# Copying the first sixteen right half rows of a half-matrix swap in uneven 4 KB strips

## The chip, the core and the metric

The kernel runs on one core of a Trainium2 chip. The metric is the device time of one execution in microseconds. The kernel uses no compute engine: it consists of copies from device memory to device memory. Two instruction queues issue them, that of SyncE (SP) and that of ScalarE (ACT), and the core's 16 DMA engines carry them out.

## The reference

The input is a matrix of 8192 x 8192 float32 numbers (268 MB). The output is the same matrix with both axes rotated by half their length, so that the four quadrants change places diagonally:

```python
def reference(x):            # x: (8192, 8192) float32
    return np.fft.ifftshift(x)
```

## The kernel before

R and C are 8192, hr and hc are 4096. A row of the output consists of a left and a right half row, each of 4096 numbers or 16 KB that lie together. The source of an output half row is the half row that lies hr rows and hc columns away (modulo the size). So the whole job is 16384 copies of 16 KB.

`ENGINES` is 16 and `per` is 16, so `rows` is 256: one DMA copies 256 half rows, 4 MB. The helper `copy(queue, row, col, dims)` issues one DMA at L29. It computes the source's place from the output's row and column, and uses the same list of steps and counts, `dims`, on both sides. The list is `back`:

```python
back = [[C, ENGINES], [-ENGINES * C, per], [1, hc]]
```

The outermost step has the count 16 and goes from one row to the next, one row for each DMA engine. The second goes back by 16 rows, 16 times: within a DMA each engine takes every sixteenth row of the block, from the block's end to its start. The innermost runs along one half row, which is one packet of 16 KB.

The outer loop takes `first` from the matrix's end to its start in steps of four blocks (1024 rows). Within a step `n` counts down from 3 to 0. SP's queue copies the left half of block n, and ACT's queue the right half of block (n + 2) % 4. The blocks of the first step of ACT are therefore 1, 0, 3, 2 of the last 1024 rows. The block with which ACT begins starts at row R - 3 * rows.

There are 64 DMAs, 32 from each queue. The framework gives them eight completion semaphores in turn, and an issue waits until the earlier DMA on its semaphore has landed. As built, ACT's issues use semaphores 0, 2, 4 and 6, SP's use 1, 3, 5 and 7. So each queue issues four DMAs at once, and each further one when its own fourth-last has landed. A DMA counts as landed when all 16 DMA engines have reported their part. No DMA depends on another one's data.

Of the kernel before, what the change touches and what calls it, by code (L numbers as in the profile page):

```python
# [1 line left out]

# [4 lines left out]


ENGINES = 16


@with_exitstack
def kernel(
    ctx: ExitStack,
    tc: tile.TileContext,
    x: bass.AP,
    out: bass.AP,
):
    nc = tc.nc
    R, C = x.shape  # L20
    hr = R // 2
    hc = C // 2
    per = 16
    rows = ENGINES * per

    def copy(queue, row, col, dims):

        src = (row + hr) % R * C + (col + hc) % C
        queue.dma_start(  # L29
            out=bass.AP(out.tensor, out.offset + row * C + col, dims),  # L30
            in_=bass.AP(x.tensor, x.offset + src, dims),
        )

    back = [[C, ENGINES], [-ENGINES * C, per], [1, hc]]

    for first in range(R - 4 * rows, -1, -4 * rows):
        for n in (3, 2, 1, 0):
            copy(nc.sync, first + n * rows + rows - ENGINES, 0, back)
            copy(nc.scalar, first + (n + 2) % 4 * rows + rows - ENGINES, hc, back)


# [1 line left out]
_INS = ['x']  # L43
_OUTS = [((8192, 8192), 'float32')]


def kernel(**inputs):
    import numpy as _np
    import concourse.bacc as _bacc
    import concourse.tile as _tile  # L50
    from concourse import mybir as _mybir
    from concourse.bass_utils import run_bass_kernel_spmd as _run

    nc = _bacc.Bacc("TRN2", target_bir_lowering=False, num_devices=1)  # L54
    arrays, args = {}, []
    for name in _INS:
        a = _np.ascontiguousarray(inputs[name])
        if a.dtype.kind in "iu":
            a = a.astype(_np.int64)
        arrays[f"in_{name}_dram"] = a  # L60
        args.append(nc.dram_tensor(f"in_{name}_dram", a.shape, _mybir.dt.from_np(a.dtype), kind="ExternalInput").ap())
    for i, (shape, dtype) in enumerate(_OUTS):
        dt = _mybir.dt.from_np(_np.dtype(dtype))
        args.append(nc.dram_tensor(f"out_{i}_dram", shape, dt, kind="ExternalOutput").ap())
    with _tile.TileContext(nc) as tc:
        kernel(tc, *args)
    r = _run(nc, [arrays], core_ids=[0])
    got = tuple(r.results[0][f"out_{i}_dram"] for i in range(len(_OUTS)))
    return got[0]
```

## Time and profile before

| What | Value |
|---|---|
| Median of 3 runs | 814.51 us (814.3 to 814.64) |
| Profiled execution | 813.9 us |
| Its span, first to last instruction | 812.1 us |
| Data moved | 268.44 MB, mean 331 GB/s |
| DMA issues | 64, of 4096 KB each |
| Issue to landing, median | 101.0 us |

The profile's rate counts each byte once. Reading and writing together are 661 GB/s. The two queues appear in it as q1 and q10. "DMA share" is the busy time of the 16 DMA engines, as a part of a stretch. "L65" in the waits is the end of the program, where it waits for the last transfers.

### The profile page before, as it was taken

Reading aid. Unit: us, or ns where it says so; the run is one execution under the profiler, and the core shown is the slowest. Engines: PE = TensorE matmul, PEld = TensorE weight load, DVE = VectorE, ACT = ScalarE, POOL = GpSimd, SP = SyncE. Lnnn points to the kernel's source line nnn. Section 1 sums busy time; section 2 is a strip of 40 time slices with the busy share of each in tenths; the row PEclk is TensorE's granted clock in tenths of the full one; section 3 lists DMA queues with packets and bytes.
Section 4 is the critical chain, followed back from the end, with each engine's and each line's share of the span. In section 5 each row is a group of like instructions: output and inputs, shape, how many; then the busy total and the mean of one; then the engine's idle time right before and its main releaser. Section 6 shows DMA issues by size and latency. Waiting matters only on the chain. (4 is left out here: it accounts for less than half of the span.)

```text
span 812.1 us, 109 instructions
## 1 busy us (share of the span) xinstructions
POOL 0.2 (0%) x4
## 2 busy tenths in 40 slices
POOL 0000000000000000000000000000000000000000
DMA  9999999999999999999999999999999999999998
GB/s 306 332 329 337 333 332 335 328 324 337 329 336 337 332 334 334 334 336 331 332 329 330 337 328 334 339 331 333 332 320 333 330 331 330 336 332 337 334 333 286
DMA packets 17408, 268.44 MB, mean 331 GB/s; under 512 B 1024, under 2 KB 1024, under 8 KB 1024
## 3 DMA queue, kind: packets, MB, share of 16 engines
q1 hardware_dynamic: 8704, 134.22, 49.9%
q10 hardware_dynamic: 8704, 134.22, 49.1%
HBM read 268.44 MB, written 268.44 MB: 661 GB/s over the span
## 5 line engine op out<-in xcount | busy, mean ns | idle before, releaser
L54 POOL MEMSET const-bfloat16-1.0<- 128x1 bf16 x1 | 0.1, 102 | 0.0
L54 POOL MEMSET const-uint8-127<- 128x1 uint8 x1 | 0.1, 102 | 0.0
L54 POOL MEMSET const-float32-1.0<- 128x1 f32 x1 | 0.1, 99 | 0.0
L54 POOL MEMSET const-float32-0.0<- 128x1 f32 x1 | 0.1, 98 | 0.2 <-issue 0.2
## 6 DMA issues: line engine op xcount, KB each, us to landing
out_dram<-in_x_dram ACTq DMA_DIRECT2D x32, 4096.0 KB, 101.0
out_dram<-in_x_dram SPq DMA_DIRECT2D x32, 4096.0 KB, 101.0
```

The costliest lines, as they stand in the source:

```text
L54: nc = _bacc.Bacc("TRN2", target_bir_lowering=False, num_devices=1)
```

## The change

ACT's first copy took 256 right half rows of the block that starts at `start` = R - 3 * rows, from the block's end to its start. Its first sixteen half rows, one for each DMA engine, are now copied separately, before everything else. They are cut into four strips of 1024 columns, 4 KB a row. Three strips go in two DMAs each: 14 rows and 2 rows, 9 and 7, 4 and 12. The fourth goes in one DMA of 16 rows. ACT's large copy of that block then does the remaining 15 times 16 half rows (`rest`); all other copies stay as they were.

So ACT issues 39 DMAs instead of 32. The seven small ones come first on its queue. If each row of a small DMA goes to a DMA engine of its own, counted from the first one, the sixteen engines get 7, 7, 6, 6, 5, 5, 5, 4, 4, 3, 3, 3, 2, 2, 1 and 1 strips; each had one half row, four strips' worth, before.

The eight semaphores are given out in the program's order. The seven strips take 0 to 6, SP's first large copy takes 7. As built, ACT's first four large copies wait for the strips on 0, 2, 4 and 6 (14, 9, 4 and 16 rows). SP's second, third and fourth copies wait for the strips on 1, 3 and 5 (2, 7 and 12 rows), and its fifth for its first. After that each queue again waits for its own fourth-last DMA.

```diff
+    start = R - 3 * rows
+    strip = hc // 4
+    for n, k in enumerate((14, 9, 4)):
+        col = hc + n * strip
+        copy(nc.scalar, start + rows - ENGINES, col, [[C, k], [1, strip]])
+        copy(nc.scalar, start + rows - ENGINES + k, col, [[C, ENGINES - k], [1, strip]])
+    copy(nc.scalar, start + rows - ENGINES, hc + 3 * strip, [[C, ENGINES], [1, strip]])
+
     back = [[C, ENGINES], [-ENGINES * C, per], [1, hc]]
-
+    rest = [[C, ENGINES], [-ENGINES * C, per - 1], [1, hc]]
     for first in range(R - 4 * rows, -1, -4 * rows):
         for n in (3, 2, 1, 0):
             copy(nc.sync, first + n * rows + rows - ENGINES, 0, back)
-            copy(nc.scalar, first + (n + 2) % 4 * rows + rows - ENGINES, hc, back)
+            right = first + (n + 2) % 4 * rows
+            if right == start:
+                copy(nc.scalar, right + rows - 2 * ENGINES, hc, rest)
+            else:
+                copy(nc.scalar, right + rows - ENGINES, hc, back)
```

## The prediction

> **What bounds the kernel now.** I read the page's summary of slices and queues first, then the queue's own waits, then the line that issues the copies, and last the windows at the two ends and along the middle. No compute engine works (POOL 0.2 us of 812.1), so the chain that ended last says nothing here; the transfer rows carry it. From the page:
>
> ```profile
> DMA  9999999999999999999999999999999999999998
> GB/s 306 332 329 337 333 332 335 328 324 337 329 336 337 332 334 334 334 336 331 332 329 330 337 328 334 339 331 333 332 320 333 330 331 330 336 332 337 334 333 286
> DMA packets 17408, 268.44 MB, mean 331 GB/s; under 512 B 1024, under 2 KB 1024, under 8 KB 1024
> q1 hardware_dynamic: 8704, 134.22, 49.9%
> q10 hardware_dynamic: 8704, 134.22, 49.1%
> HBM read 268.44 MB, written 268.44 MB: 661 GB/s over the span
> ```
>
> The sixteen DMA engines are busy in all 40 slices; the two queues share them evenly (49.9% and 49.1%, together 99%). Only the first slice (306) and the last (286) fall off. 17408 packets are 16384 half rows of 16 KB and 1024 small ones that signal completion (64 DMAs times 16). The span is therefore 16384 / 16 = 1024 half rows per DMA engine at 99% of 812.1 / 1024 = 0.785 us each. The packet records give the same: mean 784 ns, least 608, longest near 2.3 us. The least is an undisturbed packet; the 176 ns above it are contention, and that alone is what a change of phase could touch.
>
> Now who waits. These are SP's queue waits, then what all instructions of the copy's line show:
>
> ```profile
> SPq L29 <- DMA out_dram<-in_x_dram: 689.7, 28, 25.2
> SPq L65 <- DMA out_dram<-in_x_dram: 101.6, 2, 79.3
> ...
> L29 ACTq DMA_DIRECT2D out_dram<-in_x_dram x32: 577/578/884, 0.7 to 713.4; - x32
> L29 SPq DMA_DIRECT2D out_dram<-in_x_dram x32: 571/571/666, 0.7 to 709.0; - x32
> ...
> DMA to landing us min/median/max: 25.4/101.0/103.2
> ```
>
> SP waits 28 times for a DMA four places back, 689.7 us in total, and issues the next in 571 ns. Each transfer lands a median 101 us after its issue: four are outstanding on each queue, and each queue issues only once in some 25 us, so issuing is well covered. Next the start and the end: transfers of the stretches 0 to 5 us and 807 to 809 us by queue, then rates by window (microseconds, POOL busy, clock, DMA share, GB/s; a packet counts where it starts, so a short window can pass 1.00):
>
> ```profile
> q1 hardware_dynamic: 64, 1.05, 58.6%
> ...
> q10 hardware_dynamic: 39, 0.56, 91.1%
> q1 hardware_dynamic: 7, 0.00, 0.2%
> ...
> 2.20:5.00 2.80, 0.00 (x0) 1.00 1.00 363
> 12.00:25.00 13.00, 0.00 (x0) 1.00 0.99 325
> 50.00:100.00 50.00, 0.00 (x0) 1.00 1.00 337
> 250.00:300.00 50.00, 0.00 (x0) 1.00 0.99 334
> 600.00:650.00 50.00, 0.00 (x0) 1.00 1.00 328
> 700.00:750.00 50.00, 0.00 (x0) 1.00 1.00 333
> 808.00:809.00 1.00, 0.00 (x0) 1.00 0.75 197
> 809.00:810.00 1.00, 0.00 (x0) 1.00 0.31 131
> ```
>
> SP's queue (q1; its DMAs land first) moves alone until 5 us: first packet at 2.18 us, ACT's at 5.08, though both were issued at 0.73. At the end ACT's queue (q10) is alone, and the engines finish one by one between 808.7 and 810.9 us. In the middle, fifteen windows of 50 us lie between 328 and 337 GB/s, mean 332.6, without a trend.
>
> **The change, part by part.** The sum is made against the profiled execution: 813.9 us, that is a span of 812.1 and 1.8 around it. The median of the runs, 814.5, stands 0.6 above it.
>
> *Bytes and packets.* The same 268.44 MB. Sixteen packets of 16 KB become 64 of 4 KB, with 64 small ones for seven more DMAs. The trace has no 4 KB packet. Between the rows for 4 B (9 ns) and 16 KB (608 ns) a straight line gives 159 ns; four are 636 in place of 608, and four extra signals per engine 36: 0.06 us per engine. Upper bound: every strip suffers the full 176 ns that a 16 KB packet does, 4 x 335 = 1.34 against 0.784: 0.56 us. Lower bound: a quarter of 608 each, no change. I take **+0.1**, near the straight line, since the strips run while only one other stream is live.
>
> *Seven more issues on ACT.* The first issues took 0.67 to 0.88 us, and followed one another at about 0.7: seven take 4.9 us. ACT's large copy, now 15 rows per engine, goes out near 5.7 us and its packets start near 10 instead of 5.08. What hides this is SP's first DMA: 16 half rows per engine from 2.18 us, at no less than 0.61 each, so until 12 us at least, with 2.5 us of strips beside it. Without that cover it would cost the 4.9 us. Queued behind the strips on ACT are its 32 large copies; the first four of these wait for strips, and SP's second to fifth copies for strips two, four, six and its own first copy. All those strips land long before 12 us, so nobody starves: cost **0**, upper bound 1 us if ACT's descriptors come as late after their issue as in the before (4.35 us) and SP's later ones get in front.
>
> The Trainium skill's page "DMA: Bandwidth & Descriptors", section "Rules for kernel authors", speaks against this part: small transfers are to be merged, as below 64 KB one pays mostly overhead. By its table of measured sizes (0.68 us for 4 KB, 0.95 for 64 KB) seven strips in a row would be an estimated 6 us if exposed; the row of q1 above, engines fed by the other queue, says they are not.
>
> *The lag of the two streams.* SP is alone for longer, and so is ACT at the end. Before, SP got 64 / 16 = 4 half rows per engine ahead. With ACT's bulk at 10 us it gets about (10 - 2.2 - 0.6) / 0.67 = 11, less the one that the strips cover: 6 more than before, at each end. Counted by each packet's share in a stretch, they run at some 390 GB/s from 3 to 5 us, 0.67 us each, from 806 to 808 at some 370, against 0.79 with both. Were that due to the lone stream, 12 half rows x 0.12 = 1.4 us would be saved; if it is a start and an end effect, nothing. One-microsecond windows scatter widely: I take **-0.4**.
>
> *Unlike amounts.* With one row per engine, counted from the first, engines get 7,7,6,6,5,5,5,4,4,3,3,3,2,2,1,1 strips. The mean is 4, what each had before. The first two carry 12 KB too much: 12.3 KB at 331 / 16 = 20.7 GB/s is 0.59 us, or 3 x 159 ns = 0.48. It costs this in full if these engines are the last anyway, and less if a lighter one is: between -0.59 and +0.59, and as the kernel ends with its slowest engine, I take **+0.3**.
>
> *The middle.* Would unlike starts change the 784 ns? Two readings say no. Completions of one DMA over the 16 engines spread 1.1 to 1.6 us for the first four DMAs, 2.2 to 2.5 for the last four, while the windows show no trend: engines drift apart by more than a half row without becoming faster. And from 3 to 5 us they start almost together, and run fastest. One reading says yes: sorting stretches of 5 us by how far the running packets are in step, those less in step are faster, but weakly (correlation 0.22); in-step-ness itself is forgotten within 1 us (autocorrelation 0.05). I take **0**; the windows set the bounds, 328 and 337.
>
> The same page, section "Latency and other measured facts", holds a rule for the change: copies with a row pitch of 512 KiB run at 207 GB/s, of 4 MiB at 103, and padding the latter by 4 KiB gives 214; the page infers that streams in step meet in the same channel. The pitch here is 32 KB and the rate 331, and no run here shows such a collapse. By that rule, at its extreme, every packet could come down to its least, 608 ns, an estimated 632 us; by the rows of the middle the sum gets nothing.
>
> Sum: 813.9 + 0.1 + 0 - 0.4 + 0.3 + 0 = 813.9, no change; at the median 814.5.
>
> **The rivals.** *Forecast* (0.52): the middle keeps its pace, and only ends move; its own range is 813.0 to 816.2. *Faster* (0.26): engines keep their spacing over the run and meet less often. For it: the weak sorting above, and that spacing of one DMA's completions grows by only 1 us in 800, so a spacing that is set at the start could last. Against: the loss of step within 1 us. Price: the mean rises from 332.6 to 334.5 GB/s, as several windows have: 0.57% or 4.6 us, 809.9. *Slower* (0.20): ACT's stream runs 6 half rows per engine further behind, so the two streams read and write other pairs of row blocks at any moment over the whole run. For it: windows at 328 and 330 show that some pairings are worse; against: no trend. It decides once the mean is below 331.9 (0.2%); at 331, half way to the worst windows, it is 0.48% or 3.9 us: 818.4. *The change doesn't do what it says* (0.02): small DMAs aren't dealt a row per engine; then the amounts are other ones, and the time is that of the forecast or, if seven or nine rows share an engine, 8 x 0.159 = 1.3 us more.
>
> **How the numbers follow.** A measurement of this kernel tells about 0.2%, 1.6 us, from no change. The forecast's case lies almost wholly within that: with its edges same 0.50, faster 0.28, slower 0.22. The range takes in the faster rival at 809.9 and most of the slower one: 809.5 to 818.0.
>
> **What would show it.** Right: 71 issues on L29, 39 from ACT; about 17520 packets, 1152 of them under 8 KB; q10 with packets soon after 2.2 us, its 16 KB ones from some 10 us on; SP's wait near 690 us; windows of 50 us around 332.6; a lone q10 at the end for 3 to 4 us longer than now. Wrong, term by term: a window before 15 us below 300 GB/s (cover failed); last engines ending over 3 us apart (the amounts add up); every window of the middle at 334 or more, or at 331 or less (a rival).

## The result, and the profile after

The changed kernel took 811.4 us (median of 18 runs, 809.33 to 814.68) and the kernel before 814.15 us in the same comparison (18 runs, 810.02 to 817.91): ratio 0.9968, 95% interval 0.9955 to 0.9981. Three more comparisons on other chips gave 0.9982 (0.9969 to 0.9996), 0.9989 (0.9970 to 1.0007) and 0.9989 (0.9972 to 1.0006). Weighted by the inverse squares of their intervals' widths the four are 0.9980 (0.9972 to 0.9987): 1.6 us less, just where a measurement begins to tell it from no change. The three later ones alone give 0.9986 (0.9977 to 0.9995). The other chips run both kernels about 1% slower (before: 822 us), so only ratios within a chip are compared below. All comparisons on one chip share the same runs of the kernel before (29 to 35), so an error of these runs is in all of them.

The profiled execution took 812.7 us, its span is 810.9. First the page's rows for the slices and the queues:

```profile
GB/s 302 328 335 329 334 333 331 331 335 330 326 331 329 331 335 330 332 332 337 335 336 333 333 337 330 334 335 331 336 331 333 335 334 335 333 330 336 333 338 296
DMA packets 17520, 268.44 MB, mean 331 GB/s; under 512 B 1088, under 2 KB 1088, under 8 KB 1152
q1 hardware_dynamic: 8704, 134.22, 49.7%
q10 hardware_dynamic: 8816, 134.22, 49.6%
```

The packets are the foreseen ones: 64 strips under 8 KB, 64 more completion signals. The first slice is no better than before (302, it was 306); the last is (296, it was 286). Next SP's queue waits, the size and landing of the one strip DMA that uses all sixteen engines, and the queues from 16.5 to 20.5 us:

```profile
SPq L29 <- DMA out_dram<-in_x_dram: 686.8, 28, 28.4
...
out_dram<-in_x_dram ACTq DMA_DIRECT2D x1, 64.0 KB, 10.8
...
q10 hardware_dynamic: 77, 1.26, 97.4%
q1 hardware_dynamic: 17, 0.08, 5.8%
```

From 16.5 to 20.5 us SP's queue is all but empty. The text ahead of the prediction, and the prediction after it, had the semaphores wrong. By the issue records SP's first copy took the second semaphore, not the eighth, so SP's second copy waited for its first, which landed at 19.23 us, and was issued at 19.25. The nine-row, four-row and sixteen-row strips held SP's next three copies, and the fourteen-row, two-row, seven-row and twelve-row strips ACT's first four, not the ones named. It cost nothing, since ACT's large copy was there. These are the windows of the start (microseconds, POOL busy, clock, DMA share, GB/s):

```profile
5.00:10.00 5.00, 0.00 (x0) 1.00 1.04 337
10.00:15.00 5.00, 0.00 (x0) 1.00 1.02 333
15.00:20.00 5.00, 0.00 (x0) 1.00 1.00 333
20.00:25.00 5.00, 0.00 (x0) 1.00 0.96 315
25.00:30.00 5.00, 0.00 (x0) 1.00 1.02 334
```

There is no hole. Up to 50 us 15.70 MB had been moved, before 15.66: 0.1 us of gain at most. The middle, from 50 to 780 us, of the kernel before and then of the changed one:

```profile
50.00:780.00 730.00, 0.00 (x0) 1.00 1.00 333
```

```profile
50.00:780.00 730.00, 0.00 (x0) 1.00 1.00 333
```

To whole GB/s the same in this pair. Counted from the packet records it is 332.5 before and 332.7 after, which is 0.5 us over 730. The end differs more. Here are the stretches from 5 to 3 and from 3 to 1 us before the end of the span, before and then after:

```profile
807.10:809.10 2.00, 0.00 (x0) 1.00 0.89 270
809.10:811.10 2.00, 0.00 (x0) 1.00 0.16 66
```

```profile
805.90:807.90 2.00, 0.00 (x0) 1.00 0.94 319
807.90:809.90 2.00, 0.00 (x0) 1.00 0.32 115
```

Before, in the second stretch, the engines are busy for a sixth of the time: most have finished and wait for a few. After, for a third. By the completion records of the last DMA, the last engine ended 1.33 us behind the mean of the sixteen before, and 0.82 after.

### The profile page after: what moved, and what is told of

Its sections match the earlier page's. It is cut to its first block, busy times and chain, and to the rows that moved or that the text cites. A ratio compares the mean times of both kernels' runs of the same rounds, so it can differ in the third digit from the quotient of the medians.

```text
span 810.9 us, 116 instructions
## 1 busy us (share of the span) xinstructions
POOL 0.2 (0%) x4
```

## The experiments

Three theories were set against each other. A: the unlike amounts keep the engines apart. B: SP's stream leads ACT's by more, so other blocks meet all along. C: the gain is made at the start and the end, where one stream runs alone. Later D: the order of issues and semaphores does it. "Lead" is SP's bytes minus ACT's, in half rows per engine, at 400 us of the profile: 3.5 before, 5.4 after.

**First chip of three: the changed kernel again, and three that part strips, amounts and lead.**

e1_same is the changed kernel.

> The changed kernel once more, as the yardstick for the three others on this chip. All theories: 2 to 3.5 us below the kernel before (ratio 0.9957 to 0.9975), SP's stream 5 to 6 half rows per engine ahead of ACT's in the middle of the run where it was 3.5 before.

Measured: 821.31 us, ratio 0.9982 (0.9969 to 0.9996), lead 5.0: 1.7 us below before, less than was expected.

e2_even7 makes the amounts equal:

```diff
-    strip = hc // 4
-    for n, k in enumerate((14, 9, 4)): ...
+    strip = hc // 8
+    for n in range(7):
+        wide = strip if n < 6 else 2 * strip
+        copy(nc.scalar, start + rows - ENGINES, hc + n * strip, [[C, ENGINES], [1, wide]])
```

> Seven small DMAs again, but each of all 16 rows (six of 2 KB and one of 4 KB a row): same number of issues and same order of semaphores, no unlike amounts. Theory A (unlike amounts keep the engines apart): the gain is gone, within 1 us of the kernel before. Theory B (ACT's stream starts later, so SP leads by some two half rows more for the whole run): the gain stays, 2 to 3.5 us below, as the lead will be 5 half rows or more. Theory C (the gain is made in the first 30 us and at the end, by stretches with one live stream): it stays too, and the middle is at the pace of before.

Measured: 821.25 us, ratio 0.9986 (0.9973 to 0.9999), lead 7.8. The gain did not go with the unlike amounts, against A; but its last engine, 1.83 us behind the mean, ended later than before's (1.33), so it was worth repeating.

e3_even16 cuts the first half rows into 16 even strips:

```diff
-    strip = hc // 4
-    for n, k in enumerate((14, 9, 4)): ...
+    strip = hc // 16
+    for n in range(16):
+        copy(nc.scalar, start + rows - ENGINES, hc + n * strip, [[C, ENGINES], [1, strip]])
```

> The first sixteen half rows in 16 even strips of 1 KB: ACT's bulk starts later still. A: no gain, and up to 1 us lost to more issues. B: the lead grows beyond 6 half rows and the time goes further, some 1 us from the changed kernel either way. C: more of the start with one stream, 3 to 5 us below the kernel before.

Measured: 829.31 us, ratio 1.0083 (1.0063 to 1.0103), lead 24.1. All theories missed. The windows of its start:

```profile
10.00:15.00 5.00, 0.00 (x0) 1.00 0.96 315
15.00:20.00 5.00, 0.00 (x0) 1.00 0.09 26
20.00:25.00 5.00, 0.00 (x0) 1.00 0.84 276
```

Here the hole opens which the changed kernel avoids. By the issue records ACT's ninth strip shares its semaphore with SP's first copy: it was issued at 16.79 us, when that copy had landed at 16.77. SP's second copy shares one with ACT's tenth strip, which landed at 19.35, and was issued at 19.37. So each queue waited for the other with almost nothing under way; ACT's bulk was issued at 21.83 and moved its first packet at 29.3. The missing share is (329 - 26) / 329 x 5 = 4.6 us and (329 - 276) / 329 x 5 = 0.8 us: 5.4 us. The median lost 6.3 (822.99 to 829.31), this execution, which took 827.86, some 4.9.

e4_lead has no strips; one half row per engine goes from SP to ACT:

```diff
+    copy(nc.scalar, R - ENGINES, 0, [[C, ENGINES], [-ENGINES * C, 1], [1, hc]])
...
+            if left == R - rows:
+                copy(nc.sync, R - 2 * ENGINES, 0, rest)
```

> No strips at all. ACT copies the first sixteen of SP's half rows as a first DMA, and SP's first block begins one half row per engine further on: SP's stream leads by two half rows more over the whole run, 5.5 in place of 3.5, with equal amounts on all engines and the start of before. A: no gain, within 1 us of before. B: the full gain, 2 to 3.5 us. C: at most 0.5 us, from the longer lone stream at the end.

Measured: 823.32 us, ratio 1.0007 (0.9990 to 1.0024). ACT's short first DMA got its packets out first, at 2.14 us, so the lead in bytes was only 2.4. In place it is 4.4, since SP's stream begins one half row further on and one of ACT's was not of its own stream: short of the 5.5 meant. No gain, but a weak test of B.

**Second chip: the amounts enlarged, and the order of issues alone.**

> The changed kernel a third time, for a joint interval and a further profile. All theories: ratio 0.996 to 0.9985. Theory A (unlike amounts) and B (longer lead of SP's stream) put the gain into the middle, theory C into the last 30 us, so its end (from 780 us on, beyond the time that the bytes left need at the pace of the middle) shows under 0.6 us lost where before lost 0.9.

Measured (the changed kernel): 821.77 us, ratio 0.9989 (0.9970 to 1.0007), a little less gain than expected. From 780 us on it moved 12.55 MB, at its middle pace of 329.4 GB/s worth 38.1 us, in 38.9: 0.8 us lost, so not below the 0.6 that was expected.

> Seven even small DMAs once more, since the first time left both open (ratio 0.9973 to 0.9999). A: joint ratio with the first time nearer to 1 than to the changed kernel's. B and C: the same ratio as the changed kernel's on this chip, within 0.1%.

Measured (even strips once more): 821.65 us, ratio 0.9990 (0.9979 to 1.0001); joint with the first 0.9988 (0.9980 to 0.9997).

f3_rows4 splits whole half rows as the change splits strips:

```diff
-        copy(nc.scalar, start + rows - ENGINES, col, [[C, k], [1, strip]]) ...
+        row = start + rows - (n + 1) * ENGINES
+        copy(nc.scalar, row, hc, [[C, k], [1, hc]])
+        copy(nc.scalar, row + k, hc, [[C, ENGINES - k], [1, hc]])
```

> The same split of 14 and 2, 9 and 7, 4 and 12, 16, but of whole half rows of 16 KB (the first 64 half rows of ACT's block): the amounts differ by up to six half rows in place of six strips. A with spacing in time: a larger gain than the changed kernel's, 4 us or more. A with fractions of a packet only: none. If the unequal shares stay with their engines to the end, the first two engines end 3 x 0.78 = 2.3 us behind the mean and the kernel is 1 to 3 us slower than before. B: SP's lead is about that of before (full packets), so no gain.

Measured: 822.72 us, ratio 1.0015 (1.0000 to 1.0030), lead 2.2. The large amounts do not help the middle, which speaks against a spacing in time. What they do is seen at the end:

```profile
814.60:816.60 2.00, 0.00 (x0) 1.00 0.53 213
816.60:818.60 2.00, 0.00 (x0) 1.00 0.14 57
```

Already five to three microseconds before the end nearly half of the engine time is gone. The sixteen engines ended over 5.17 us (2.0 to 3.8 in the kernels with equal amounts); their amounts differed by six half rows, 6 x 0.79 = 4.7 us. The completion records show it all along. A queue that shares the engines gets half of their time (49.9% and 49.1% before), so six half rows in ACT's queue are 6 x 1.57 = 9.4 us: its large copies between the first and the last landed over 8.0 to 9.9 us from the first engine to the last (1.1 to 2.9 before), SP's copies, which have equal amounts, over 1.2 to 2.4. On average over ACT's middle sixteen copies the landings lie from 4.4 us before their mean to 4.6 behind it, where the dealt amounts give 4.7 either way. An unequal share that is given at the start is thus still there 800 us later. The last engine ended 2.09 us behind the mean, where 2.3 was expected.

f4_issue7 replaces the seven strips with seven DMAs of one whole half row per engine:

```diff
-    for n, k in enumerate((14, 9, 4)): ...
+    for n in range(7):
+        copy(nc.scalar, start + rows - (n + 1) * ENGINES, hc, [[C, ENGINES], [1, hc]])
```

> ACT's first block begins with seven DMAs of one half row per engine (16 KB packets, equal amounts), then the remaining nine: seven more issues and the order of semaphores of the changed kernel, SP's second DMA waiting for its first, but no small packets. A: no gain. B: the lead stays near 3.5 half rows or less, so no gain. If the changed order of the issues is what helps (theory D), the gain is here too, ratio 0.9965 to 0.998.

Measured: 821.01 us, ratio 0.9991 (0.9975 to 1.0007), lead 0.4. Theory D had given 0.9965 to 0.998; the interval is compatible with D and with no gain.

**Third chip: the noise, four even strips, and the mirror.**

> The changed kernel a last time, for the joint interval with the three earlier comparisons (0.9968, 0.9982, 0.9989). All theories: ratio 0.9965 to 0.999.

Measured (the changed kernel): 820.73 us, ratio 0.9989 (0.9972 to 1.0006).

> The kernel before, compared with itself: shows how far a ratio strays with nothing changed, and gives a second profile of before, on a chip of the experiments. All theories: the ratio's interval holds 1. Theory C (the end): the end from 780 us on again loses 0.9 us or more against the pace of the middle.

Measured: 823.12 us against 821.60, ratio 1.0019 (0.9998 to 1.0040). Nothing was changed, and 0.19% appears, with the interval just holding 1. So a single ratio of 0.998 or 1.002 is no finding. Its end: 13.25 MB after 780 us, 40.4 us at 328.4 GB/s, took 41.6: 1.2 us lost, as C expected.

g3_even4 has four even strips of 4 KB:

```diff
-    for n, k in enumerate((14, 9, 4)): ...
+    for n in range(4):
+        copy(nc.scalar, start + rows - ENGINES, hc + n * strip, [[C, ENGINES], [1, strip]])
```

> Four even strips of 4 KB, each one DMA of all 16 rows: the strips and the mean number of them per engine as in the changed kernel, equal amounts, three issues fewer. A (unlike amounts): within 0.05% of before. B (longer lead): SP leads by 5 half rows or more in the middle, and the ratio is the changed kernel's, within 0.1%. C (lone streams at the ends): the same, with an end like the changed kernel's.

Measured: 822.22 us, ratio 1.0003 (0.9986 to 1.0021), lead 9.4. The lead is longer than the changed kernel's and the gain is not there: against B. Its runs are 1.4 us (0.5 to 2.3, from both kernels' runs) above the changed kernel's of the same chip. It is the only comparison in which even strips were slower: e2_even7 and the changed kernel had 821.25 and 821.31, f2_even7 and the changed kernel 821.65 and 821.77. On average of these two chips seven even strips and the unlike ones are equal, 0.7 us either way. The end of g3_even4, and then that of the changed kernel on that chip (g1_same):

```profile
816.20:818.20 2.00, 0.00 (x0) 1.00 0.81 295
818.20:820.20 2.00, 0.00 (x0) 1.00 0.14 57
```

```profile
816.10:818.10 2.00, 0.00 (x0) 1.00 0.87 287
818.10:820.10 2.00, 0.00 (x0) 1.00 0.29 107
```

With the same strips and equal amounts the last stretch is half as busy. In e2_even7, as fast as the changed kernel, the stretch from 3 to 1 us before the end is emptier still (0.08, 33 GB/s).

g4_mirror has the change's split on SP's queue:

```diff
-    start = R - 3 * rows
+    start = R - rows
...
-        copy(nc.scalar, start + rows - ENGINES, col, [[C, k], [1, strip]]) ...
+        copy(nc.sync, start + rows - ENGINES, n * strip, [[C, k], [1, strip]]) ...
...
+            if left == start:
+                copy(nc.sync, left + rows - 2 * ENGINES, 0, rest)
```

> The changed split on SP's queue in place of ACT's: SP's first sixteen left half rows in strips of 14 and 2, 9 and 7, 4 and 12, 16, so that ACT's stream leads by some five half rows and SP's ends last. A: the changed kernel's gain, ratio 0.9965 to 0.999. B: the pairing of blocks is another one, so no gain is promised, up to 0.2% either way. C: the changed kernel's gain, as the ends have a lone stream as long.

Measured: 820.71 us, ratio 0.9992 (0.9974 to 1.0010), just outside the 0.9965 to 0.999 that A and C gave. The lead turned and became large (ACT 21.3 half rows ahead), as SP's large copy shared a semaphore with ACT's first and was issued only at 17.35 us. Yet the time is that of the changed kernel on this chip, within 0.1 us (0.9 either way). Whatever the lead does, it does not order these times. Its end is the busiest of all, and before it SP's queue runs alone from 801.2 us on, long enough to read the pace of a lone stream (first line):

```profile
802.00:814.00 12.00, 0.00 (x0) 1.00 0.99 333
816.20:818.20 2.00, 0.00 (x0) 1.00 0.44 139
```

From 700 to 780 us, with both streams, this execution moved 331 GB/s. In e3_even16 ACT's queue is alone from 804.8 us: 330 GB/s from 806 to 820, and 330 from 700 to 780. So a lone stream is not faster, against C.

All of them side by side; the last column is how far the last engine ended behind the mean of the sixteen, from the completion records:

| Kernel | Amounts | Lead | Ratio to before | Last engine, us |
|---|---|---|---|---|
| before, and g2_null | equal | 3.5, 3.2 | 1, 1.0019 | 1.33, 1.52 |
| changed (4 profiles) | 7 to 1 strips | 5.0 to 5.8 | 0.9968, 0.9982, 0.9989, 0.9989 | 0.82, 1.02, 0.94, 0.94 |
| g4_mirror | 7 to 1 strips | -21.3 | 0.9992 | 0.59 |
| e2, f2_even7 | equal | 7.8, 7.9 | 0.9986, 0.9990 | 1.83, 1.57 |
| g3_even4 | equal | 9.4 | 1.0003 | 1.59 |
| e3_even16 | equal | 24.1 | 1.0083 | 1.26 |
| f4_issue7 | equal | 0.4 | 0.9991 | 0.90 |
| e4_lead | equal | 2.4 | 1.0007 | 2.48 |
| f3_rows4 | 7 to 1 half rows | 2.2 | 1.0015 | 2.09 |

What follows: with unlike amounts in strips the engines ended closer together, 0.93 us behind the mean (four profiles of the changed kernel) against 1.43 (two of before) and 1.66 (three with even strips of 2 or 4 KB). The nine profiles with strips at the start fall into two groups without overlap, 0.59 to 1.02 with unlike amounts and 1.26 to 1.83 with equal ones. Each is one execution, and it is not the only thing that sets the end: f4_issue7 ended at 0.90 with equal amounts, e4_lead at 2.48. Counted in bytes it is the same: in the four microseconds from 5 to 1 before the end the four profiles moved 832 KB on average, the two of before 639 KB, which is 0.58 us at 330 GB/s.

So the end would account for some 0.5 us of the joint 1.6, but the times do not confirm it: the two kernels of seven even strips, whose ends are no better than before's, have a joint ratio of 0.9988, and the changed kernel on the three later chips has 0.9986. Theory D stays open as a rival. On the later chips the kernels with seven small DMAs ahead of a bulk have 0.9982 to 0.9992, all but f3_rows4 with its long end (1.0015); those with fewer, g3_even4, e4_lead and g2_null, have 1.0003 to 1.0019. No run took the order of issues and semaphores apart from the number of small DMAs, and these differences are hardly larger than the noise.

The other microsecond was not located. It is not in the start. In the first pair the middle holds 0.5 us of it, but on the third chip g3_even4, which gained nothing, had a faster middle in its profile than the changed kernel (329.0 against 328.8 GB/s), so one profile each cannot tell. And it is of the size that g2_null strayed with nothing changed.

## Why the prediction was right or wrong

*The whole.* 814.5 us was forecast, with 813.0 to 816.2 for the likeliest case, no change. 811.4 lies inside the range and outside that case, 0.32% below before, where 0.28 of the chance stood. The joint ratio, 0.20% below, lies on the border, and the three later chips alone, 0.14% below, lie within no change. That the first number fell inside the range is partly luck: the lower bound was set by the faster rival, whose rise of the middle did not appear.

*Packets.* The straight line gave 159 ns for a strip. In the packet records the median of the 64 is 159 ns and the mean 185. With the signals the term is 0.06 us by the median and 0.17 by the mean; 0.1 was taken.

*Seven issues.* Expected in 4.9 us with ACT's bulk starting near 10 us; they took from 0.73 to 6.5, the first alone 1.42 us, and the bulk's first packet came at 12.9. The strips' first packet came at 5.03 us, not soon after 2.2. The "2.5 us of strips" beside SP's first copy is an error of the sum: four strips of 159 ns are 0.64 us per engine. The term 0 held, but only in part by its argument. SP's first copy did cover ACT's bulk, but SP's second copy waited for it, and the strips landed as late as 16.7 us. From then to 20.5 us the cover was ACT's bulk beside an all but idle SP queue, and e3_even16 shows what it costs when both are missing: 5.4 us. The sign set for a failed cover, a window under 300 GB/s before 15 us, does occur (294 from 8 to 12 us, after 375 from 5 to 8), but so it does in the kernel before (295 from 8 to 10 us): over so short a stretch it tells nothing. By the table in the section "Bandwidth" of the Trainium skill's page "DMA: Bandwidth & Descriptors", which is for loads into on-chip memory issued from GpSimd, seven small DMAs were an estimated 6 us if exposed. The windows from 5 to 20 us show 333 to 337 GB/s with them: unexposed, they cost nothing that the rate shows.

*The lag.* Six half rows more were expected at both ends. The lead did rise to 13 at 15 us, but SP's pause gave most of it back: 2 more remained for the run. At the end ACT's queue was alone for 4.5 us, before for 2.9: 1.6 us longer, where 3 to 4 were expected. The term of -0.4 us had no ground: a lone stream that lasts 12 to 14 us runs at 333 and 330 GB/s (g4_mirror, e3_even16), no faster than two. The 370 to 390 GB/s of the short stretches were an effect of the start and the end, as the prediction itself had allowed. With 0 here, and -0.5 for the unlike amounts as the ends have it, the terms would add up to -0.4 us of the joint -1.6: that the sum came to no change rests on two terms that were off and partly cancel.

*Unlike amounts.* This step failed, by the profiles of the end, in its sign. It took +0.3 us of a possible -0.59 to +0.59, arguing that the kernel ends with its slowest engine. The premise that the amounts last to the end was right, as far as whole half rows show (f3_rows4). But the end became closer by 0.5 us, near the other bound, so the heavier engines can hardly have been the late ones. That is inferred: the records carry no engine number, why the engines with the most strips would otherwise be early is not shown, and the times of the even strips do not confirm that the closer end saves time. The Trainium skill's page "DMA: Bandwidth & Descriptors", section "Why a DMA increments its semaphore by 16 and not by 1", states that a copy on fewer than 16 engines takes the lowest-numbered ones. No run here shows the numbers, but the landings of f3_rows4 fit a sum of shares that all start with the same engine.

*The middle.* 0 was taken, and 333 GB/s stood before and after (332.5 and 332.7). The faster rival's rise to 334.5 over the middle did not appear, nor the slower one's fall to 331. The rival that engines keep their spacing and so meet less often had its premise right, as spacing put in at the start stays, and its effect not: spacing six half rows wide left the time at 1.0015.

## What to carry to other kernels

When a copy keeps all DMA engines busy, the last microseconds are what a static split may still change: look at the busy share of the last two or three. An unequal share given at the very start is still there at the end, so it can be sized by the spread of the last completions; which engines should get more, these records could not say, and a saving in time was not shown. Before putting small DMAs ahead of large ones, list which earlier DMA each copy waits for: in e3_even16 two queues waited for each other through shared semaphores and lost some 5 us. Before reading anything into 0.2%, compare the kernel with itself.

## What the runs showed of the hardware

- Unequal shares of the DMA engines did not even out in 800 us of common work (f3_rows4): 4.7 us put in, landings of one queue's copies 8.0 to 9.9 us apart all along while two queues ran, 5.17 us of spread at the end.
- A copy stream from one queue alone moved as much as two streams together: 333 against 331 GB/s in g4_mirror, 330 against 330 in e3_even16.
- Small DMAs beside large packets on the other queue move slowly: 64 strips of 159 ns each, 0.64 us per engine, took ACT's queue from 5.0 to 16.1 us. The last of their DMAs had been issued by 6.5 us.
- The executions of the kernel before scatter more than those of the changed one: on the three later chips standard deviations of 1.72 us (99 runs) and 1.12 us (35 runs). Over all kernels there, starts in pieces under 16 KB gave 1.15 (the changed one, e2 and f2_even7, g3_even4, g4_mirror; e3_even16 with its hole left out), starts in whole half rows 1.78. The gain in the median goes with before's longer executions; its shortest ones there are no longer than the changed kernel's (818.59 to 819.94 us before, 819.83 to 820.55 after, of about a third as many runs). On the first chip the deviations are 1.85 and 1.55 us (18 runs each). Why was not tried.
